# The first layer's modulation vectors as TensorE matmuls, and all low parts on VectorE

## The chip, the cores and the metric

The kernel runs on one core of a Trainium2 chip. The metric is the time of one execution on the device in microseconds (us). The core's engines are TensorE (PE, with its weight loads as PEld), VectorE (DVE), ScalarE (ACT) and GpSimd (POOL); SyncE (SP) issues most of the transfers.

## The reference, cut to what matters

Two blocks follow each other on 256 tokens of width 1024. The first is one layer of spatial gating, attention and a mixture of experts. The second has two layers on the same tokens and on 256 context tokens, each of them a feed-forward part, a mixer and a second feed-forward part. Each layer of the second block is steered by nine modulation vectors of 1024 numbers for each of two conditions, `c` and `c_ctx`:

```
mx = jnp.split(jax.nn.silu(c) @ ada_w[layer] + ada_b[layer], N_MOD, axis=-1)
mc = jnp.split((jax.nn.silu(c_ctx) @ ada_w[layer] + ada_b[layer])[None, :], N_MOD, axis=-1)
x = x + 0.5 * mx[2][:, None] * swiglu(modulate(rms_norm(x), mx[0], mx[1]), ...)
...
def modulate(h, shift, scale):
    return h * (1 + scale[:, None, :]) + shift[:, None, :]
```

`ada_w` is [2, 1024, 9216] in float32. A layer's share is 72 tiles of 512 KB, multiplied by only two vectors. All else in the reference is the same before and after.

## The kernel before, in words

**Weights in two parts.** Every weight block is a tile of 128x1024 float32 (512 KB). `W` (lines 101 to 115) loads it on SP's queue into `raw`. ScalarE copies it to `whi`, rounded to float32r (line 113), and the low part `wlo` is `raw - whi` (line 114), on VectorE or on GpSimd by a pattern of zeros and ones (`P1`, `PA`, `PB`, `PC` and so on, one for each stage). Three matmuls (lines 139 to 141) then make up one product. There are 5 buffers of `raw`, 6 of `whi` and 5 of `wlo`. A block serves 24 matmuls of 256 columns or 12 of 512 columns when 256 tokens are worked on, and twice these columns for 512 tokens.

**Stages.** By the profile's time: block 1 (0 to 400 us; the projections `w_in` and `w_u`, attention beside the first half of the gated merge, the second half, `w_out`), with the first feed-forward part of the context tokens begun at its end; the mixture of experts (to about 800 us; 32 experts with 4 blocks of `w13` and 2 of `w2` each, the context's feed-forward steps emitted between them); then of the second block's layer 0 the feed-forward part on `x` (827 to 1074 us), the mixer and the second feed-forward part over 512 tokens; then the same of layer 1, the last feed-forward part on 256 tokens alone (2227 to 2416 us).

**Modulation.** `ada(L)` (lines 832 to 875) is a generator of 72 steps. A step loads a tile `araw` of transposed `ada_w` (line 847, two buffers); GpSimd multiplies it by the condition `cb[:, 1]` into `ajk` (line 851) and ScalarE sums the rows (line 852); VectorE does product and sum for `cb[:, 0]` in one instruction (line 855). The sums are columns of `acols`. After 24 steps the bias is added and the gate rows go to scratch memory. Steps are emitted beside the main work: `W` pumps `rate` steps for each block (`R1`, `RA`, `RC`), and `need` makes up what a stage must have.

**Order.** A scheduler with a simulated time line places the instructions of each engine. Each engine and SP's queue then run in that order; an instruction that waits holds back what stands behind it. Copies of activations into `cols` (lines 838 and 845; at steps 0, 24 and 48 of layer 1, at steps 24 and 48 of layer 0 through `GT`) keep the steps behind them from being placed earlier than those activations.

**Banks.** PSUM tiles by tag: three `mm`, two `at`, two `tr` and one `ada`. The `ada` bank is also the output of attention in block 1 and in the mixers.

Of the kernel before, what the change touches and what calls it, by code (L numbers as in the profile page):

```python
# [6 lines left out]
F32 = mybir.dt.float32  # L7
F32R = mybir.dt.float32r
# [3 lines left out]
OP = mybir.AluOpType  # L12
# [18 lines left out]
PF = (1,1)  # L31
# [3 lines left out]
P1 = (0,0,0,0,0,1)  # L35
PM = (0,)
PA = (0,0,0,1)
PB = (0,1,1,1)
PC = (1,)
# [4 lines left out]
P2 = (0,1,1)  # L44
PN = (0,1,1)
PM0 = (0,1)
# [23 lines left out]
class Builder:  # L70
# [7 lines left out]
    # ------------------------------------------------------------ tiles  # L78
# [38 lines left out]
    def pump(self, n):  # L117
        """emit n steps of the work that runs beside the main chain"""
        while self.side and n > 0:
            try:  # L120
                next(self.side[0])
                n -= 1
                self.done += 1
            except StopIteration:
                self.side.pop(0)

    def need(self, L, third):
        """the modulation of layer L, up to a third, has been emitted"""
        self.pump(72 * L + 24 * third - self.done)
# [5 lines left out]
    def mm3(self, p, L, R, first, last):  # L135
        """p (+)= (Lh + Ll)^T (Rh + Rl) without the product of the two low parts."""
# [23 lines left out]
        # y <- (y * y * v * s - 3) * y = -2 * next, with the scale s of the step before  # L160
# [11 lines left out]
    def row_norm(self, x, i, g=None, use=None):  # L172
        """x[:, i] * its reciprocal root mean square (* g), in a scratch tile; use is called for each half"""
# [17 lines left out]
    def half(self, x, i):  # L191
        """the first half of the sum for a norm, before the second half of the row is there"""
# [57 lines left out]
    # ------------------------------------------------------------ program  # L250
# [45 lines left out]
    def proj_T(self, p, wb, c, hh, hl, ts, kts=range(8)):  # L296
        """p[d, tokens] of one tile of 128 output columns, weights stationary"""
# [5 lines left out]
    def block1(self):  # L303
# [3 lines left out]
        with tc.tile_pool(name="b1", bufs=1, reuse_waits="tile") as P:  # L307
# [43 lines left out]
            # w_in blocks, moving form, 4 per 512 columns: v_a 0.., k 8.., q 16.., v_b 24..  # L351
# [38 lines left out]
            # lam = exp(q1.k1) - exp(q2.k2) + 0.2  # L390
# [9 lines left out]
            # constants of the query / key / sub norms: gain * hd**-0.5, gain * (1 - lam_init)  # L400
# [5 lines left out]
            # ---- q, k, v_b  # L406
# [27 lines left out]
            # ---- differential attention  # L434
# [3 lines left out]
            def attention():  # L438
                for tt in range(2):
# [54 lines left out]
            # ---- gated merge, channel-major  # L494
# [12 lines left out]
                        # 2 sigmoid(z) = 1 + tanh(z / 2)  # L507
# [23 lines left out]
            # the context tokens' first norm  # L531
# [9 lines left out]
            # ---- x += merged @ w_out  # L541
# [7 lines left out]
    # ------------------------------------------------------------ mixture of experts  # L549
# [751 lines left out]
def prep(I):  # L1301
# [3 lines left out]
    D = {}  # L1305
# [91 lines left out]
```

## Time and profile before

| | |
|---|---|
| median of 3 runs | 2422.49 us (2419.78 to 2427.06) |
| the profiled execution: span from first to last instruction | 2426.3 us |
| its time apart from the span | not listed; the span lies among the three runs |
| mean granted TensorE clock | 0.955 |
| PE, DVE, ACT, POOL busy | 90%, 73%, 50%, 45% of the span |
| moved by DMA | 438.04 MB, mean 181 GB/s |

The busy share of an engine is a mean over stages that have different limits. The page's slices show PE at seven tenths and above nearly everywhere, DMA at nine tenths in the experts' stage only, VectorE at eight or nine tenths in block 1, the experts and the stage after them, and GpSimd busy mostly where the modulation steps run. The granted clock falls below full speed in slices where TensorE had pauses.

### The profile page before, as it was taken

The page shows a single profiled execution, that of the slowest core. Times are in us where ns is not written, and L with a number is a line of the kernel's source. Part 1 is how long each engine was busy: PE and PEld are TensorE (multiplying, and loading weights), DVE is VectorE, ACT ScalarE, POOL GpSimd, SP SyncE. Part 2 cuts the span into 40 slices and gives each one's busy share as a digit, 9 for nine tenths or more (in the row PEclk, how much of TensorE's full clock was granted, in tenths as well). Part 3 has the DMA queues.
Part 4 walks back from the last instruction along what each step waited for, and adds up shares of the span by engine and source line. Part 5 has one row for each costly group of instructions (what it writes and reads, how often), then busy time and mean ns, then how long its engine had stood idle before and what let it go on. Part 6 is the DMA issues. An engine that isn't in the chain of part 4 may idle for free. (4 is left out here: it accounts for less than half of the span.)

```text
span 2426.3 us, 32703 instructions
## 1 busy us (share of the span) xinstructions
PE 2185.9 (90%) x11890; PEld 1789.9 (74%) x11890; DVE 1762.7 (73%) x2334; ACT 1219.1 (50%) x1926; POOL 1096.8 (45%) x528
## 2 busy tenths in 40 slices
PE   7778899999999788878998999899989999888998
PEld 5657787757666677666877878688768888767997
DVE  7899878898898799999657787755874343764334
ACT  6445545888888554444635434333542222444443
POOL 5656141000000366674136989963661101414885
PEclk9899899999999899988999999999999999988999
DMA  7564365899999666663123445443453222312553
GB/s 274 168 211 154 113 215 174 315 336 326 338 322 338 244 212 232 224 203 129 49 97 130 166 156 191 171 142 105 161 169 113 96 87 87 124 66 97 187 186 114
DMA packets 121924, 438.04 MB, mean 181 GB/s; under 512 B 15072, under 2 KB 15200, under 8 KB 121632
## 3 DMA queue, kind: packets, MB, share of 16 engines
q1 hardware_dynamic: 113760, 413.19, 49.6%
q0 software_dynamic: 8000, 22.73, 2.7%
q8 instruction: 94, 1.54, 0.3%
q14 instruction: 70, 0.57, 0.1%
HBM read 429.52 MB, written 6.34 MB: 180 GB/s over the span
## 5 line engine op out<-in xcount | busy, mean ns | idle before, releaser
L114 POOL TENSOR_TENSOR wlo<-raw,whi 128x1024 fp32r<-128x1024 f32 x233 | 606.4, 2617 | 540.7 <-PE mm L141 155.3
L113 ACT ACTIVATE whi<-raw 128x1024 fp32r<-128x1024 f32 x640 | 666.1, 1054 | 325.5 <-PE mm L141 115.2
L114 DVE TENSOR_TENSOR wlo<-raw,whi 128x1024 fp32r<-128x1024 f32 x407 | 570.4, 1411 | 128.9 <-PE mm L141 55.3
L851 POOL TENSOR_TENSOR ajk<-araw,cb 128x1024 f32<-128x1024 f32 x144 | 417.2, 2897 | 288.0 <-DMA araw<-ada_w 166.9
L855 DVE SCALAR_TENSOR_TENSOR araw<-araw,cb 128x1024 f32<-128x1024 f32 x144 | 311.5, 2164 | 85.4 <-POOL ajk L851 85.4
L852 ACT ACTIVATE ajk<-ajk 128x1024 f32<-128x1024 f32 x144 | 152.3, 1058 | 261.9 <-POOL ajk L851 256.0
L140 PE MATMUL mm<-wlo,fh 128*128 128x512 f32 x616 | 247.7, 405 | 20.2 <-DVE wlo L114 13.0
L139 PE MATMUL mm<-whi,fh 128*128 128x512 f32 x616 | 246.5, 406 | 13.2 <-ACT fh L132 8.7
L141 PE MATMUL at<-hT,wlo 128*128 128x256 f32 (+1 forms) x736 | 247.5, 338 | 7.1 <-DVE wlo L114 7.1
L141 PE MATMUL mm<-whi,fl 128*128 128x512 f32 x616 | 246.5, 403 | 7.1 <-DVE fl L133 7.0
L140 PE MATMUL mm<-hT,whi 128*128 128x256 f32 (+1 forms) x736 | 245.7, 335 | 8.0 <-DVE hT L133 8.0
L139 PE MATMUL at<-hT,whi 128*128 128x256 f32 (+1 forms) x736 | 245.7, 338 | 7.9 <-DVE silu L928 7.9
L141 PE MATMUL mm<-hT,wlo 128*128 128x256 f32 (+1 forms) x736 | 244.7, 334 | 4.6 <-DVE wlo L114 4.6
L140 PE MATMUL at<-hT,whi 128*128 128x256 f32 (+1 forms) x736 | 247.3, 337 | 0.0
L139 PE MATMUL mm<-hT,whi 128*128 128x256 f32 (+1 forms) x736 | 243.2, 336 | 2.5 <-ACT hT L132 2.5
L694 POOL DMA_DIRECT2D yo<-os x64 | 31.8, 497 | 378.7 <-ACT os L693 364.2
L133 DVE TENSOR_TENSOR fl<-silu,fh 128x256 fp32r<-128x256 f32 (+1 forms) x104 | 135.8, 1309 | 48.2 <-ACT fh L132 48.2
L928 DVE TENSOR_TENSOR silu<-silu,at 128x256 f32<-128x256 f32 (+1 forms) x104 | 54.9, 528 | 147.5 <-PE at L141 144.9
L141 PEld LDWEIGHTS at<-hT,wlo 128*128 128x128 f32 x736 | 143.2, 195 | 22.5 <-DVE wlo L114 7.9
L139 PEld LDWEIGHTS at<-hT,whi 128*128 128x128 f32 x736 | 142.1, 195 | 23.5 <-DVE silu L928 8.1
L140 PEld LDWEIGHTS mm<-wlo,fh 128*128 128x128 f32 x616 | 118.7, 193 | 55.1 <-DVE wlo L114 17.5
L140 PEld LDWEIGHTS mm<-hT,whi 128*128 128x128 f32 x736 | 140.5, 191 | 24.4 <-DVE hT L133 10.0
(369 smaller groups left out, 4631.6 us busy)
## 6 DMA issues: line engine op xcount, KB each, us to landing
raw<-gu SPq DMA_DIRECT2D x220, 512.0 KB, 4.4
raw<-w SPq DMA_DIRECT2D x192, 512.0 KB, 5.2
araw<-ada_w SPq DMA_DIRECT2D x144, 512.0 KB, 3.8
raw<-dn SPq DMA_DIRECT2D x110, 512.0 KB, 4.5
raw<-w_in SPq DMA_DIRECT2D x54, 512.0 KB, 4.6
raw<-w_out SPq DMA_DIRECT2D x24, 512.0 KB, 4.1
raw<-w_gate SPq DMA_DIRECT2D x16, 512.0 KB, 4.4
raw<-w_up SPq DMA_DIRECT2D x16, 512.0 KB, 3.8
```

The source lines that it names most:

```text
L113: self.nc.scalar.activation(out=hi[:, :cols], in_=src, func=AF.Copy)
L114: eng.tensor_tensor(out=lo[:, :cols], in0=src, in1=hi[:, :cols].bitcast(F32), op=OP.subtract)
L133: self.nc.vector.tensor_tensor(out=lo, in0=src, in1=hi.bitcast(F32), op=OP.subtract)
L139: mm(p, lh, rh, start=first, stop=False)
L140: mm(p, lh, rl, start=False, stop=False)
L141: mm(p, ll, rh, start=False, stop=last)
L694: (nc.scalar if YS else nc.gpsimd).dma_start(yo[e * CAP : e * CAP + CAP, c * 512 : c * 512 + 512], os)
L851: nc.gpsimd.tensor_tensor(out=jk, in0=raw, in1=cb[:, 1], op=OP.mult)
L852: nc.scalar.activation(out=jk, in_=jk, func=AF.Copy, accum_out=acc[1])
L855: nc.vector.scalar_tensor_tensor(out=raw, in0=raw, scalar=1.0, in1=cb[:, 0], op0=OP.mult, op1=OP.mult, accum_out=acc[0])
L928: nc.vector.tensor_tensor(out=s, in0=s, in1=pgu[1][c], op=OP.mult)
```

## The change

1. **Low parts.** All patterns become `(0,)`: the 233 subtractions that GpSimd did go to VectorE. GpSimd keeps a copy of keys in the mixers and the issue of transfers.
2. **Layer 0's modulation on TensorE.** Four tiles of `ada_w0` (4 x 256 rows by 512 columns) make a group; there are 18 groups. Eight float32 matmuls take 32 stationary columns (the two conditions and 30 zeros) and 512 moving columns. They write to four partition ranges of one `ada` bank in turn (kt % 4), so that each range holds a part of the sum. ScalarE copies the bank to `e`, four small matmuls with the selection matrix `c_sel` add the parts and turn rows into columns, and one VectorE addition brings the bias.
3. **Layer 1's modulation on VectorE alone.** Both products with sums are VectorE instructions (lines 862 and 863 of the changed kernel). The conditions `cb` are loaded when layer 1 begins, into two of the `araw` buffers.
4. **Buffers.** `araw` has five buffers in place of two; `cb`, `ajk` and `arow` are gone and their contents use the ring of `araw`, as do two key tiles and a query tile in the mixers.
5. **Copies.** The copies at steps 24 and 48 of layer 0 (`GT`) are gone; layer 1 keeps its own.
6. `need` rounds up to whole groups of four steps. Comments are removed throughout, which shifts line numbers.

```diff
-PF = (1,1)
+PF = None
-P1 = (0,0,0,0,0,1)
+P1 = (0,)
...
-GT = (24,48)
...
     def need(self, L, third):
-        self.pump(72 * L + 24 * third - self.done)
+        n = max(72 * L + 24 * third, self.done)
+        self.pump(n + -n % 4 - self.done)
...
     def ada_begin(self):
-        self.cb = self.t(G, [128, 2, 1024], F32, "cb")
-        for a in range(2):
-            nc.gpsimd.dma_start(self.cb[:, a], self.A["c_rows"][a].partition_broadcast(128))
-        nc.scalar.activation(out=self.cb, in_=self.cb, func=AF.Silu)
+        self.cc = self.t(G, [128, 8, 32], F32, "cc")
+        nc.vector.memset(self.cc, 0.0)
+        c = self.load(G, "c_cols", [128, 8, 2], "ccol")
+        nc.scalar.activation(out=self.cc[:, :, 0:2], in_=c, func=AF.Silu)
+        self.sel = self.load(G, "c_sel", [128, 2], "csel")
...
         if L:
+            cb = [self.t(G, [128, 1024], F32, "araw", 5) for _ in range(2)]
+            for a in range(2):
+                nc.gpsimd.dma_start(cb[a], A["c_rows"][a].partition_broadcast(128))
+                nc.scalar.activation(out=cb[a], in_=cb[a], func=AF.Silu)
...
         for n in range(72):
-            if n in (GT, GT1)[L]:
+            if L and n in GT1:
...
-            raw = self.t(G, [128, 1024], F32, "araw", 2)
-            nc.sync.dma_start(raw, A["ada_w"][L, n])
-            jk = self.t(G, [128, 1024], F32, "ajk")
-            acc = [cols[:, a, n : n + 1] for a in range(2)]
-            if PF and n % PF[1] < PF[0]:
-                nc.gpsimd.tensor_tensor(out=jk, in0=raw, in1=cb[:, 1], op=OP.mult)
-                nc.scalar.activation(out=jk, in_=jk, func=AF.Copy, accum_out=acc[1])
+            raw = self.t(G, [128, 1024], F32, "araw", 5)
+            nc.sync.dma_start(raw, A["ada_w0"][n] if L == 0 else A["ada_w"][n])
+            if L == 0:
+                pend.append(raw)
+                if n % 4 == 3:
+                    self.ada_rows(cols, b, n // 4, pend)
+                    pend = []
             else:
-                nc.vector.scalar_tensor_tensor(out=jk, in0=raw, scalar=1.0, in1=cb[:, 1], op0=OP.mult, op1=OP.mult, accum_out=acc[1])
-            nc.vector.scalar_tensor_tensor(out=raw, in0=raw, scalar=1.0, in1=cb[:, 0], op0=OP.mult, op1=OP.mult, accum_out=acc[0])
+                jk = self.t(G, [128, 1024], F32, "araw", 5)
+                nc.vector.scalar_tensor_tensor(out=jk, in0=raw, scalar=1.0, in1=cb[1], op0=OP.mult, op1=OP.mult, accum_out=cols[:, 1, n : n + 1])
+                nc.vector.scalar_tensor_tensor(out=raw, in0=raw, scalar=1.0, in1=cb[0], op0=OP.mult, op1=OP.mult, accum_out=cols[:, 0, n : n + 1])
...
+    def ada_rows(self, cols, b, g, wf):
+        p = self.mm([128, 512], "ada")
+        for kt in range(8):
+            r = slice(kt % 4 * 32, kt % 4 * 32 + 32)
+            nc.tensor.matmul(p[r], self.cc[:, kt], wf[kt // 2][:, kt % 2 * 512 : kt % 2 * 512 + 512], start=kt < 4, stop=kt >= 4)
+        e = self.t(self.G, [128, 512], F32, "araw", 5)
+        nc.scalar.activation(out=e, in_=p, func=AF.Copy)
+        q = self.mm([128, 4, 2], "ada")
+        for c in range(4):
+            nc.tensor.matmul(q[:, c], e[:, c * 128 : c * 128 + 128], self.sel, start=True, stop=True)
+        k = slice(4 * g, 4 * g + 4)
+        nc.vector.tensor_tensor(out=cols[:, :, k], in0=q.rearrange("p c a -> p a c"), in1=b[:, None, k].to_broadcast([128, 2, 4]), op=OP.add)
```

The scheduler gives another order. Of layer 0's 72 tiles, 24 were loaded in block 1 and 48 after the experts; now 28 are loaded before the experts' stage gets going, 40 between its first 55 weight blocks, and 4 late in layer 0's mixer. SP's queue at the start of the experts, before (`w` are blocks of `w13` and `w2`, `gu` and `dn` those of the context's feed-forward part, `araw` the modulation tiles):

```order
L112 DMA raw<-gu 128x1024 x12
L112 DMA raw<-dn 128x1024 x3
L112 DMA raw<-w 128x1024 x5
L779 TENSOR_LOAD mxi
L779 ISA x2
L112 DMA raw<-w 128x1024 x3
L112 DMA raw<-dn 128x1024 x3
L112 DMA raw<-w 128x1024 x12
L112 DMA raw<-gu 128x1024 x4
```

The same place of SP's queue in the changed kernel:

```order
L111 DMA raw<-dn 128x1024
L854 DMA araw<-ada_w 128x1024 x4
L111 DMA raw<-dn 128x1024
L854 DMA araw<-ada_w 128x1024
L111 DMA raw<-w 128x1024
L854 DMA araw<-ada_w 128x1024 x3
L111 DMA raw<-w 128x1024 x6
L854 DMA araw<-ada_w 128x1024 x4
L111 DMA raw<-w 128x1024 x5
L854 DMA araw<-ada_w 128x1024
L111 DMA raw<-gu 128x1024
L854 DMA araw<-ada_w 128x1024 x3
```

In this manner it goes on to the 40th tile; behind it the queue of the experts is as before. On TensorE's own order in the changed kernel, these tiles' matmuls (`ada<-araw,cc`) stand mostly in pairs between the experts' matmuls:

```order
L139 MATMUL mm<-whi,hd 32x512
L891 MATMUL ada<-araw,cc 32x512 x2
L140 MATMUL mm<-wlo,hd 32x512
L141 MATMUL mm<-whi,hd 32x512
L139 MATMUL mm<-whi,hd 32x512
L140 MATMUL mm<-wlo,hd 32x512
L141 MATMUL mm<-whi,hd 32x512
L891 MATMUL ada<-araw,cc 32x512 x2
L145 MATMUL tr<-ident,hs 128x32 x2
```

Before, no modulation work stood between them on any engine. In layer 0's feed-forward part on `x` it is the other way round. SP's queue before, from that part's start:

```order
L112 DMA raw<-gu 128x1024 x2
L847 DMA araw<-ada_w 128x1024
L112 DMA raw<-gu 128x1024
L847 DMA araw<-ada_w 128x1024
L112 DMA raw<-gu 128x1024 x3
L847 DMA araw<-ada_w 128x1024
L112 DMA raw<-dn 128x1024
L847 DMA araw<-ada_w 128x1024
```

and in the changed kernel, from the same start up to the mixer's `w_out`:

```order
L111 DMA raw<-gu 128x1024 x6
L111 DMA raw<-dn 128x1024 x8
L111 DMA raw<-gu 128x1024 x16
L111 DMA raw<-dn 128x1024 x8
L111 DMA raw<-gu 128x1024 x12
L111 DMA raw<-dn 128x1024 x6
L111 DMA raw<-w_in 128x1024 x12
L111 DMA raw<-w_out 128x1024 x6
L854 DMA araw<-ada_w 128x1024
```

All of that part's modulation tiles have left it. Layer 1's steps stay in layer 0's second and layer 1's first feed-forward part, and there VectorE's order in the changed kernel has both products of a tile (lines 862, 863) next to the low parts (line 113):

```order
L862 SCALAR_TENSOR_TENSOR araw,acols<-araw 128x1024
L113 TENSOR_TENSOR wlo<-raw,whi 128x1024
L863 SCALAR_TENSOR_TENSOR araw,acols<-araw 128x1024
L862 SCALAR_TENSOR_TENSOR araw,acols<-araw 128x1024
L863 SCALAR_TENSOR_TENSOR araw,acols<-araw 128x1024
L952 TENSOR_TENSOR silu<-silu,at 128x512
L862 SCALAR_TENSOR_TENSOR araw,acols<-araw 128x1024
L133 TENSOR_TENSOR fl<-silu,fh 128x512
```

Before, the first of the two and the low parts of that stage were on GpSimd.

## Rows read from the trace of the kernel before

**Rows 1.** The page: busy time of each engine, share of the span, instructions.

```profile
PE 2185.9 (90%) x11890; PEld 1789.9 (74%) x11890; DVE 1762.7 (73%) x2334; ACT 1219.1 (50%) x1926; POOL 1096.8 (45%) x528
```

**Rows 2.** Windows by stage: busy us and instructions of each engine, clock, DMA share.

```profile
0.00:280.00 280.00, 211.24 (x1217) 181.00 (x1218) 245.69 (x380) 145.63 (x267) 145.25 (x71) 0.91 0.55 190
...
400.00:800.00 400.00, 381.99 (x2054) 258.13 (x2053) 352.97 (x415) 331.31 (x458) 31.79 (x64) 1.00 0.92 325
800.00:1160.00 360.00, 288.37 (x1707) 253.13 (x1706) 327.86 (x425) 172.75 (x283) 212.40 (x94) 0.90 0.58 198
1160.00:1320.00 160.00, 149.56 (x904) 127.00 (x903) 101.41 (x185) 81.28 (x184) 55.19 (x29) 0.96 0.27 85
1320.00:1840.00 520.00, 491.87 (x2186) 394.97 (x2185) 368.99 (x343) 209.97 (x315) 382.70 (x141) 0.98 0.46 157
1840.00:2080.00 240.00, 240.00 (x1028) 193.06 (x1028) 97.35 (x114) 66.78 (x85) 32.37 (x16) 1.00 0.30 97
2080.00:2240.00 160.00, 131.13 (x729) 109.04 (x728) 101.92 (x219) 73.52 (x144) 54.71 (x37) 0.87 0.28 91
2240.00:2426.00 186.00, 176.49 (x1236) 164.13 (x1234) 75.49 (x92) 79.58 (x111) 144.76 (x60) 0.98 0.49 162
```

**Rows 3.** Costliest groups of the page: xcount | busy us, mean ns | idle before, releaser.

```profile
L114 POOL TENSOR_TENSOR wlo<-raw,whi 128x1024 fp32r<-128x1024 f32 x233 | 606.4, 2617 | 540.7 <-PE mm L141 155.3
...
L114 DVE TENSOR_TENSOR wlo<-raw,whi 128x1024 fp32r<-128x1024 f32 x407 | 570.4, 1411 | 128.9 <-PE mm L141 55.3
L851 POOL TENSOR_TENSOR ajk<-araw,cb 128x1024 f32<-128x1024 f32 x144 | 417.2, 2897 | 288.0 <-DMA araw<-ada_w 166.9
```

**Rows 4.** Groups by form, VectorE, 840 to 1080 us.

```profile
L114 DVE TENSOR_TENSOR wlo<-raw,whi 128x1024 fp32r<-128x1024 f32 x44 | 83.1, 1901 | 1.1 <-PE mm L141 0.6 <-ACT whi L113 0.5
```

**Rows 5.** Groups by form, VectorE, 1320 to 1600 us.

```profile
L855 DVE SCALAR_TENSOR_TENSOR araw<-araw,cb 128x1024 f32<-128x1024 f32 x45 | 131.3, 2918 | 45.3 <-POOL ajk L851 45.3
L133 DVE TENSOR_TENSOR fl<-silu,fh 128x512 fp32r<-128x512 f32 x16 | 26.1, 1635 | 9.8 <-ACT fh L132 9.8
```

**Rows 6.** Groups by form, VectorE, 440 to 800 us.

```profile
L114 DVE TENSOR_TENSOR wlo<-raw,whi 128x1024 fp32r<-128x1024 f32 x220 | 265.7, 1219 | 40.0 <-ACT whi L113 35.9 <-ACT fh L132 0.6 <-PE at L729 0.5
```

**Rows 7.** Line 855: ns min/median/max, first and last start.

```profile
L855 DVE SCALAR_TENSOR_TENSOR araw<-araw,cb x144: 1209/1226/3495, 28.1 to 1815.8; 128x1024 f32<-128x1024 f32 x144
```

**Rows 8.** Waits of TensorE, 0 to 280 us: us in total, times, longest.

```profile
PE tr L145 <- DVE T L183: 14.3, 2, 8.4
PE mm L140 <- DVE wlo L114: 13.9, 7, 3.1
```

**Rows 9.** TensorE in order of time: start us, us, form, pieces merged.

```profile
2171.95 1.03 PE L1152 MATMUL mm<-fftc,pf 128*128 128x256 f32 x4
2172.63 0.58 PE L1096 MATMUL at<-araw,qT 128*128 128x512 f32 x1
```

**Rows 10.** The same view, 192 to 194 us.

```profile
192.43 1.10 PE L453 MATMUL at<-A,A 64*128 64x128 f32 x8
193.46 0.39 PE L140 MATMUL mm<-S,whi 128*128 128x256 f32 x1
```

**Rows 11.** The same view, 2182 to 2185 us.

```profile
2182.49 1.89 PE L1110 MATMUL ada<-v,aT 128*128 128x64 f32 x16
2184.22 0.50 PE L145 MATMUL tr<-ident,e 128*128 128x128 f32 x3
```

**Rows 12.** DMA issues: line, engine, count, KB each, us to landing.

```profile
araw<-ada_w SPq DMA_DIRECT2D x144, 512.0 KB, 3.8
```

**Rows 13.** Windows of two feed-forward passes over 256 tokens.

```profile
827.00:1074.00 247.00, 210.04 (x1337) 190.06 (x1336) 226.57 (x213) 122.61 (x194) 155.36 (x56) 0.91 0.63 213
2227.00:2416.00 189.00, 189.00 (x1327) 177.08 (x1327) 74.39 (x81) 85.66 (x118) 148.76 (x61) 0.99 0.47 157
```

**Rows 14.** Chain that ended last, 2100 to 2160 us: start us, us, what.

```profile
2118.05 2.29 DVE rsy L159
...
2128.93 2.71 DVE xs L1066
```

More of the change, by code (lines that the diff above doesn't have):

```diff
@@ L34 @@
 KD = 3
-P1 = (0,0,0,0,0,1)
+P1 = (0,)
 PM = (0,)
-PA = (0,0,0,1)
-PB = (0,1,1,1)
-PC = (1,)
+PA = (0,)
+PB = (0,)
+PC = (0,)
 PO = "ada"
@@ L43 @@
 NA = 3
-P2 = (0,1,1)
-PN = (0,1,1)
-PM0 = (0,1)
+P2 = (0,)
+PN = (0,)
+PM0 = (0,)
 R2 = .3
@@ L50 @@
 AB = 2
-GT = (24,48)
 CUT = (0,3,5,8,11)
 LAG = 1
-PU = (1,)
+PU = (0,)
 KF = 0
@@ L824, in ada_begin @@
         nc, G = self.nc, self.G
-        self.cb = self.t(G, [128, 2, 1024], F32, "cb")
-        for a in range(2):
-            nc.gpsimd.dma_start(self.cb[:, a], self.A["c_rows"][a].partition_broadcast(128))
-        nc.scalar.activation(out=self.cb, in_=self.cb, func=AF.Silu)
+        self.cc = self.t(G, [128, 8, 32], F32, "cc")
[3 more added lines that the diff above has]
+        self.sel = self.load(G, "c_sel", [128, 2], "csel")
     def ada(self, L):
         nc, A, G = self.nc, self.A, self.G
-        cb = self.cb
         d2 = self.dr.tile([2, 3, 1024], F32, tag="ada2", bufs=2, name="ada2")
@@ L841, in ada @@
         nc.gpsimd.dma_start(b, A["ada_b"][L])
+        pend = []
         for n in range(72):
-            if n in (GT, GT1)[L]:
+            if L and n in GT1:
                 gate = self.x[:, 0, 0:48] if self.gate is None else self.gate[:, 0:48]
                 nc.vector.tensor_copy(cols[:, :, n : n + 24], gate.rearrange("p (a b) -> p a b", a=2))
-            raw = self.t(G, [128, 1024], F32, "araw", 2)
-            nc.sync.dma_start(raw, A["ada_w"][L, n])
-            jk = self.t(G, [128, 1024], F32, "ajk")
-            acc = [cols[:, a, n : n + 1] for a in range(2)]
-            if PF and n % PF[1] < PF[0]:
-                nc.gpsimd.tensor_tensor(out=jk, in0=raw, in1=cb[:, 1], op=OP.mult)
-                nc.scalar.activation(out=jk, in_=jk, func=AF.Copy, accum_out=acc[1])
-            else:
-                nc.vector.scalar_tensor_tensor(out=jk, in0=raw, scalar=1.0, in1=cb[:, 1], op0=OP.mult, op1=OP.mult, accum_out=acc[1])
-            nc.vector.scalar_tensor_tensor(out=raw, in0=raw, scalar=1.0, in1=cb[:, 0], op0=OP.mult, op1=OP.mult, accum_out=acc[0])
+            raw = self.t(G, [128, 1024], F32, "araw", 5)
[4 more added lines that the diff above has]
+                    self.ada_rows(cols, b, n // 4, pend)
+                    pend = []
+            else:
+                jk = self.t(G, [128, 1024], F32, "araw", 5)
+                nc.vector.scalar_tensor_tensor(out=jk, in0=raw, scalar=1.0, in1=cb[1], op0=OP.mult, op1=OP.mult, accum_out=cols[:, 1, n : n + 1])
+                nc.vector.scalar_tensor_tensor(out=raw, in0=raw, scalar=1.0, in1=cb[0], op0=OP.mult, op1=OP.mult, accum_out=cols[:, 0, n : n + 1])
             if n % 24 == 23:
@@ L858, in ada @@
                 k = slice(24 * t, 24 * t + 24)
-                nc.vector.tensor_tensor(out=cols[:, :, k], in0=cols[:, :, k], in1=b[:, None, k].to_broadcast([128, 2, 24]), op=OP.add)
+                if L:
+                    nc.vector.tensor_tensor(out=cols[:, :, k], in0=cols[:, :, k], in1=b[:, None, k].to_broadcast([128, 2, 24]), op=OP.add)
                 k = slice(24 * t + 8, 24 * t + 16)
@@ L868, in ada @@
                     self.tr(p[:, a], cols[:, a, k])
-                r = self.t(G, [8, 2, 128], F32, "arow")
+                r = self.t(G, [8, 2, 128], F32, "araw", 5)
                 nc.scalar.activation(out=r, in_=p, func=AF.Copy)
@@ L874, in ada @@
         self.dbg(f"mods{L}", cols)
+    def ada_rows(self, cols, b, g, wf):
+        nc = self.nc
+        p = self.mm([128, 512], "ada")
[9 more added lines that the diff above has]
+        nc.vector.tensor_tensor(out=cols[:, :, k], in0=q.rearrange("p c a -> p a c"), in1=b[:, None, k].to_broadcast([128, 2, 4]), op=OP.add)
     def seg(self, cols, a, s):
@@ L967, in mixer @@
             v = self.t(P, [128, 4, 128], F32, "v")
-            kT = [self.t(self.G, [128, 2, 512], F32R, "araw", 2) for _ in range(2)]
+            kT = [self.t(self.G, [128, 2, 512], F32R, "araw", 5) for _ in range(2)]
             S = {}
@@ L1071, in queries @@
                         qr = q8
-                    qc = self.t(self.G, [128, 8, 2, 64], F32R, "ajk")
+                    qc = self.t(self.G, [128, 8, 2, 64], F32R, "araw", 5)
                     self.split(qr, qc[:, :, 0], qc[:, :, 1])
@@ L1340, in prep @@
     D["c_rows"] = np.concatenate([I["c_2"], I["c_ctx_2"][None]])
-    D["ada_w"] = np.stack([np.ascontiguousarray(w.T).reshape(72, 128, 1024) for w in I["ada_w_2"]])
+    D["ada_w0"] = mov(I["ada_w_2"][0], 512)
+    D["ada_w"] = np.ascontiguousarray(I["ada_w_2"][1].T).reshape(72, 128, 1024)
+    D["c_cols"] = np.ascontiguousarray(D["c_rows"].reshape(2, 8, 128).transpose(2, 1, 0))
+    sel = np.zeros((4, 32, 2), f)
+    sel[:, 0, 0] = sel[:, 1, 1] = 1
+    D["c_sel"] = sel.reshape(128, 2)
     D["ada_b"] = np.stack([col(v) for v in I["ada_b_2"]])
```

## The prediction, made before the changed kernel ran

> **What bounds the kernel now.** I read the page's busy times first [rows 1]: TensorE 90%, VectorE 73%, GpSimd 45%. The mean hides the stages, so the windows come next [rows 2]. In each, TensorE's busy time times its granted clock is about the work it did at full speed; the rest of the window is lost to it. For 0 to 280 us that is 280 - 211 x 0.91 = 88 us lost; for 800 to 1160, 360 - 288 x 0.90 = 100; for 1160 to 1320, 160 - 150 x 0.96 = 16; for 1320 to 1840, 520 - 492 x 0.98 = 38; for 2080 to 2240, 160 - 131 x 0.87 = 46; for the last 186 us 13. From 1840 to 2080 nothing is lost: 240 us of it hold 1028 matmuls, so one of 512 columns takes 0.233 us. The experts (400 to 800) lose 18, and there the transfers are at their limit too: share 0.92, 325 GB/s. So TensorE is the bound of the second half, TensorE and the transfers together bound the experts, and two stages, block 1 and 800 to 1160, lose 188 us of the 319.
>
> Why these two? VectorE is busy 246 of 280 us and 328 of 360 us there [rows 2], and part of that is not its own work. A low part costs it 1.22 us in the experts, where GpSimd only issues transfers [rows 6], but 1.90 us between 840 and 1080 [rows 4]. The product with sum of line 855 takes 1.21 us at least and 3.50 at most [rows 7]; between 1320 and 1600, beside a GpSimd that never rests, its mean is 2.92 and that of `fl` 1.64 [rows 5]. GpSimd needs 2.62 us for a low part and 2.90 for a product [rows 3]. Instructions with two inputs on chip are stretched while GpSimd computes. TensorE then waits for low parts and for chains of small VectorE instructions [rows 8]; in the layer-1 mixer a step on one number per partition or eight takes 2.29 us and a gain of 512 numbers 2.71 [rows 14].
>
> **What goes from GpSimd to VectorE.** 233 low parts [rows 3] at 1.22 us add 284 us to VectorE. The 407 it had cost 1.41 each; at 1.22 they give back 77. Of line 855's 144 products (2.16 us would be 311 in all; at 1.22 they are 176) the count stays 144: 72 of layer 0 go, 72 of layer 1 come. So VectorE's total hardly moves, but it moves in place: in block 1 24 products go and 25 low parts come, so its 246 us fall to some 190 of 280, and between 800 and 1160 the 43 products vanish. Bounds for the price of a low part: 1.22 with GpSimd still, 1.90 with it at work; I take 1.22, since nothing but transfers is left on GpSimd but for two key copies in each mixer.
>
> **What the 18 groups cost TensorE.** No row shows a matmul on 32 columns in float32. The nearest: a float32 matmul appears as two passes; four passes of 256 columns start 0.68 us before the next form [rows 9], three intervals of 0.216 and a rest, so a pass of 512 columns is 0.43 us. One behind the other a group's 16 passes would take 6.9 us. The nearest row for tiles of the array side by side is line 453, whose two halves use different rows of it: eight passes of 256 columns take 1.03 us [rows 10] where the spacing above gives 7 x 0.216 + 0.03 = 1.54. A third is saved: each matmul's second pass runs beside the next one's first. I take that for columns too: 16 passes 4.6 us. The four selections are eight passes of 0.108 us (16 take 1.73 [rows 11]), 0.9 us. A group is 5.5 us, 18 are 99. Ends: nothing saved, 7.8 us and 140; four at once, 1.7 + 0.9 = 2.6 us and 47.
>
> These prices rest on rows; what the Trainium skill says of it stands beside them. Its page TensorEngine Tiling (Array Packing), section Theoretical Speedup, gives up to four times for a dimension of 32; by that the 18 groups would be the 47 us end. Its section Key Properties says that changing the tiling mode drains the engine, which speaks against 32-column pairs strewn among full matmuls. The trace shows a third saved and a next matmul 1.03 us after eight passes, so neither the full factor nor a long drain; for columns no row shows either.
>
> **Block 1.** Lost now 88. Of this 14 is the first norm chain [rows 8], which stays at about 12; waits for low parts (14 by VectorE) nearly go; of the softmax and norm chains half. The clock's part, 211 x 0.09 = 19, halves as pauses go. I take 40 us back (bounds: 0, if TensorE's new waits replace the old; 60, if only start and clock stay). Six groups stand in this stage, 33 us; some wait with attention for the same `ada` bank, so I cover none. Net -7. A seventh group, at the stage's end, counts half: +3.
>
> **The experts.** Here the order puts 40 tiles, ten groups. On the transfers: 0.524 MB at 325 GB/s is 1.61 us, 64 us in all. On TensorE: ten groups, 55 us, with little lost to hide them in. Both limits are near full and grow together, so I take the larger: +64. Bounds: +32, if the share rises from 0.92 to 1.00; +90, if passes don't overlap (78) and the one `ada` bank makes groups wait for ScalarE's copy and VectorE's addition (about 1 us a group). On SP a modulation load that waits for a buffer holds back the experts' blocks behind it; five `raw` buffers stand ahead.
>
> **Layer 0's first feed-forward part.** The order leaves no modulation in it. The same 66 blocks on the same 256 tokens run at the kernel's end without any: 189 us there, 247 here [rows 13]. I take all of the difference, -58. VectorE then has its 74 us of the later pass and 66 x 1.22 = 81 for low parts, 155 of 189. Bounds: -45 if these make waits, -62.
>
> **Mixers and the rest.** The two mixers' chains lose contention: the two records above alone are over by some 2 us each, and a chain has a handful. -9 for layer 0's (its stages lose 16 and the rest of 100 - 58), -8 for layer 1's, -3 at the end; the last group, among the mixer's `w_out`, +3. Bounds for the three together -30 and +5, since low parts now stand between the links.
>
> **Layer 1's 72 tiles** (1320 to 1840): GpSimd's product goes, VectorE's doubles. The order sets 24 tiles beside 19 blocks, 1.25 a block. A block of 512 tokens is 24 x 0.233 = 5.6 us of TensorE. VectorE has 1.22 for the low part, 1.25 x 2 x 1.22 = 3.05 for products, up to 0.8 for `fl`: 5.1. It fits with 0.5 us to spare. Two `araw` buffers hold the conditions, so three are left: a tile's load starts when the products of the second tile before it end, and has one tile's period, about 4 us, for a latency of 3.8 [rows 12]. I take +3 (bounds -15 and +58, below).
>
> **Sum.** -7 + 3 + 64 - 58 - 9 - 8 - 3 + 3 + 3 = -12 us against the profiled span of 2426.3, which is 3.8 above the median 2422.5: 2414 there, 2410 for the median.
>
> **Rivals.**
> A. Four columns at once, 2.6 us a group: block 1 gets back 17, the rest 3, the experts stay with their transfers; and block 1's pauses go but for the start, 10 more. 2410 - 30 = 2380. For it: the four ranges are written in turn; against: second passes follow in the same range.
> B. Slower: VectorE becomes the bound under layer 1's tiles. It now waits itself for each tile's load (before, GpSimd did, 166.9 us of its idle time [rows 3]), and behind it stand low parts and `silu`, for which TensorE waits. The point: 0.5 us a block is free, 0.4 a tile. A load issued late on SP's queue makes the wait 1.2 us: 72 x 0.8 = 58. 2468. Against: five `wlo` buffers let TensorE run on for a while, and the tiles come in three bursts.
> C. The tiles don't run side by side as the change means them to: 7.8 us a group. Block 1 +14, the experts +24 with the bank's waits, the other two groups +4: 2452. Against: line 453's rows.
>
> **How the numbers follow.** Chances: forecast 0.50 (own range 2388 to 2430), A 0.20, B 0.16, C 0.14. A measurement of this kernel can tell about 0.3%, 7 us. Below 2415 lie two thirds of the forecast's case and nearly all of A: 0.52. Within 2415 to 2430: a quarter of the forecast's, a little of the others: 0.16. Above: 0.32. The range goes from A less 35 us, where block 1 gives all, to B: 2345 to 2468.
>
> **What would show it.** Low parts at 1.22 us everywhere; experts about 64 us longer at a share of 0.92 or more, with ten groups of 5 to 6 us of TensorE in their first third; the feed-forward part of layer 0 at 190 us; block 1 near its old length; VectorE's waits for `araw` under 0.4 us a tile. Wrong: experts that grow by under 40 or over 90, a feed-forward part over 205, or VectorE at 95% between 1320 and 1840 with TensorE waiting for low parts.

## The result, and the profile after

The changed kernel takes 2321.4 us (median; 2320.0 to 2322.2) against 2421.1 us for the kernel before on the same chip: a ratio of 0.958, 95% interval 0.957 to 0.960. The prediction had the sign, but its 2410 us is 89 us too high and the time lies below its range. The profiled execution's span is 2318.2 us, 108.1 shorter than before.

The page after answers to [rows 1, 3, 12]; its first row is the busy time of each engine, the second row is VectorE's low parts (count | busy us, mean ns | idle before), the third a transfer (count, size, us to landing):

```profile
PE 2211.2 (95%) x12322; PEld 1779.3 (77%) x12322; DVE 1548.9 (67%) x2581; ACT 1087.1 (47%) x1658; POOL 80.7 (3%) x153
...
L113 DVE TENSOR_TENSOR wlo<-raw,whi 128x1024 fp32r<-128x1024 f32 x640 | 776.5, 1221 | 275.3 <-PE mm L141 143.4
...
araw<-ada_w SPq DMA_DIRECT2D x144, 512.0 KB, 4.6
```

All 640 low parts are VectorE's, each at 1.22 us, and its total still fell by 214 us. GpSimd computes nothing to speak of.

For the stages I take marks that both traces have: block 1 ends with VectorE's last `x<-mm,x`; a feed-forward part begins with its first matmul `at<-hT` and, where a mixer follows, ends with its last down matmul. Lengths in us; "layer 1's tiles" are layer 0's second and layer 1's first feed-forward part.

| stage | before | changed | difference | predicted |
|---|---|---|---|---|
| block 1 | 348.6 | 307.6 | -41.0 | -7 + 3 |
| experts | 479.2 | 533.0 | +53.8 | +64 |
| layer 0, first feed-forward | 246.0 | 187.8 | -58.2 | -58 |
| layer 0, mixer | 214.1 | 186.4 | -27.7 | -9 + 3 |
| layer 1's tiles | 793.1 | 773.2 | -19.9 | +3 |
| layer 1, mixer | 147.1 | 132.4 | -14.7 | -8 |
| last feed-forward, end | 198.2 | 197.9 | -0.3 | -3 |
| sum | 2426.3 | 2318.2 | -108.1 | -12 |

Windows of the changed kernel, which answer to [rows 2, 13] (start:end, length, busy us of TensorE, weight loads, VectorE, ScalarE, GpSimd, clock, DMA share, GB/s):

```profile
0.00:280.00 280.00, 259.92 (x1706) 217.09 (x1707) 195.25 (x407) 149.01 (x261) 9.62 (x21) 0.98 0.61 213
308.00:841.00 533.00, 496.92 (x2731) 328.25 (x2731) 415.56 (x578) 369.11 (x513) 39.92 (x74) 0.97 0.87 313
840.00:1028.00 188.00, 188.00 (x1326) 176.07 (x1325) 116.38 (x158) 90.40 (x123) 1.60 (x3) 0.99 0.57 182
1028.00:1215.00 187.00, 180.34 (x1051) 149.92 (x1050) 122.60 (x313) 92.73 (x207) 8.26 (x17) 1.00 0.26 87
1240.00:1760.00 520.00, 507.01 (x2266) 411.62 (x2267) 363.25 (x555) 142.97 (x185) 3.11 (x6) 0.99 0.50 161
1970.00:2130.00 160.00, 141.34 (x786) 117.47 (x785) 109.11 (x266) 78.57 (x155) 11.28 (x19) 0.94 0.32 104
```

Worked as before, TensorE loses 280 - 260 x 0.98 = 25 us in the first 280 (88 before), 18 between 1240 and 1760 (38 in the matching 520), 27 in layer 1's mixer (46). What it still waits for in the first 280 us answers to [rows 8] (total, times, longest):

```profile
PE tr L145 <- DVE T L183: 8.3, 1, 8.3
PE ada L891 <- ACT cc L829: 6.2, 1, 6.2
PE ada L891 <- ACT hft L479: 1.9, 2, 1.2
```

The start is left, and the waits for low parts are gone. The small instructions of layer 1's mixer, against [rows 14]:

```profile
2021.37 0.23 DVE L159 TENSOR_SCALAR rsy<-rsv 128x8 int32<-128x8 int32 x2
...
2027.85 0.69 DVE L1090 TENSOR_TENSOR xs<-xs,qgain 128x512 f32<-128x512 f32 x1
```

Two such steps now end within 0.23 us where one took 2.29, and the gain takes 0.69 in place of 2.71. In the kernel before, the slow step stood beside low parts on GpSimd (start us, us):

```profile
2116.86 8.20 POOL L114 TENSOR_TENSOR wlo<-raw,whi 128x1024 fp32r<-128x1024 f32 x3 [0.94 <-ACT whi L113]
2117.97 2.38 DVE L159 TENSOR_SCALAR rsy<-rsv 128x8 int32<-128x8 int32 x1
```

It reads one array on chip, not two, so the prediction's sentence that instructions with two inputs on chip are stretched is true but not the whole.

A piece of a modulation group among the experts (start us, us, form, records):

```profile
410.82 0.40 PE L139 MATMUL mm<-whi,hd 128*32 128x512 f32 x1
411.15 1.05 PE L891 MATMUL ada<-araw,cc 128*32 128x512 f32 x4
412.13 0.41 PE L140 MATMUL mm<-wlo,hd 128*32 128x512 f32 x1
```

One tile's two matmuls are four passes on two ranges of columns; the next matmul starts 0.98 us later. The order places most groups in such pieces. The experts' stage holds eleven groups' matmuls: the ten whose tiles it loads, and one whose tiles were loaded before it. All 18 groups' matmuls hold TensorE 65 us from a piece's start to the next other matmul, 3.6 a group; with a selection of 0.85 that is 4.5.

### The profile page after: what moved, and what is told of

Its sections match the earlier page's. It is cut to its first block, busy times and chain, and to the rows that moved or that the text cites. A ratio compares the mean times of both kernels' runs of the same rounds, so it can differ in the third digit from the quotient of the medians.

```text
span 2318.2 us, 32701 instructions
## 1 busy us (share of the span) xinstructions
PE 2211.2 (95%) x12322; PEld 1779.3 (77%) x12322; DVE 1548.9 (67%) x2581; ACT 1087.1 (47%) x1658; POOL 80.7 (3%) x153
## 5 line engine op out<-in xcount | busy, mean ns | idle before, releaser
L113 DVE TENSOR_TENSOR wlo<-raw,whi 128x1024 fp32r<-128x1024 f32 x640 | 776.5, 1221 | 275.3 <-PE mm L141 143.4
L140 PE MATMUL at<-hT,whi 128*128 128x256 f32 (+1 forms) x736 | 244.2, 333 | 0.0
L140 PE MATMUL mm<-wlo,fh 128*128 128x512 f32 x616 | 241.4, 395 | 0.4 <-DVE wlo L113 0.3
L139 PE MATMUL at<-hT,whi 128*128 128x256 f32 (+1 forms) x736 | 241.2, 332 | 0.0
L140 PEld LDWEIGHTS mm<-hT,whi 128*128 128x128 f32 x736 | 141.3, 192 | 23.8 <-DVE hT L133 9.2
L139 PEld LDWEIGHTS mm<-hT,whi 128*128 128x128 f32 x736 | 139.1, 192 | 19.3 <-ACT hT L132 4.5
L141 PEld LDWEIGHTS mm<-hT,wlo 128*128 128x128 f32 x736 | 141.3, 192 | 14.6
L141 PEld LDWEIGHTS at<-hT,wlo 128*128 128x128 f32 x736 | 140.1, 190 | 14.7
L140 PEld LDWEIGHTS at<-hT,whi 128*128 128x128 f32 x736 | 140.1, 190 | 14.7
L139 PEld LDWEIGHTS at<-hT,whi 128*128 128x128 f32 x736 | 138.4, 190 | 14.7
L132 ACT ACTIVATE fh<-silu 128x256 fp32r<-128x256 f32 (+1 forms) x104 | 52.3, 503 | 203.6 <-DVE silu L952 203.6
L912 DVE TENSOR_TENSOR gadd<-mm,grow 128x512 f32<-128x512 f32 x100 | 68.8, 688 | 117.4 <-PE mm L141 116.5
L139 PEld LDWEIGHTS mm<-whi,fh 128*128 128x128 f32 x616 | 116.1, 188 | 30.8 <-ACT os L693 1.7
L141 PEld LDWEIGHTS mm<-whi,fl 128*128 128x128 f32 x616 | 116.1, 188 | 27.3
```

Of the source, the lines that this page charges most:

```text
L113: eng.tensor_tensor(out=lo[:, :cols], in0=src, in1=hi[:, :cols].bitcast(F32), op=OP.subtract)
L132: self.nc.scalar.activation(out=hi, in_=src, func=AF.Copy)
L139: mm(p, lh, rh, start=first, stop=False)
L140: mm(p, lh, rl, start=False, stop=False)
L141: mm(p, ll, rh, start=False, stop=last)
L912: nc.vector.tensor_tensor(out=t, in0=p, in1=g[:, cs], op=OP.mult)
```

## The experiments

Two theories stood at the start. Theory 1: VectorE freed of a computing GpSimd makes the gain. Theory 2: the first layer's products off VectorE make it. A ratio is to the kernel before on the same chip, where its median was 2421 to 2425 us; the 95% interval stands beside it.

**Low parts back on GpSimd** (changed kernel):

```
-P1 = PA = PB = PC = P2 = PN = PM0 = PU = (0,)
+P1 = (0,0,0,0,0,1); PA = (0,0,0,1); PB = (0,1,1,1)
+P2 = PN = (0,1,1); PM0 = (0,1); PC = PU = (1,)
```

> Layer 0's modulation stays on TensorE and layer 1's two products on VectorE, as in the changed kernel; only the low parts go back to the old shares between GpSimd and VectorE. Theory 1 (the gain beyond the forecast is VectorE freed of a computing GpSimd): most of it is lost again, 2370 to 2410 us, with low parts on VectorE above 1.4 us. Theory 2 (the gain is the first layer's modulation off VectorE, whatever GpSimd does): 2325 to 2345 us.

Measured 2411.1 us, ratio to before 0.995 (0.993 to 0.997): 90 of the 100 us gained are lost again, 1 us above theory 1's range. TensorE still did the first layer's modulation, so theory 2 is out. But theory 1's sign came only in part: VectorE's low parts took 1.28 us on average (1.35 in block 1, 1.44 between 1050 and 2212 us), not above 1.4. So this run doesn't tell whether VectorE was stretched or TensorE waited for GpSimd's slower low parts (2.60 us each); the run with idle work, below, goes into that.

**All low parts on VectorE, modulation as before** (kernel before, the lists at (0,)):

> The kernel before with all low parts on VectorE and nothing else: modulation as it was, its first product on GpSimd and the second on VectorE. Theory 1: some of the gain comes by this alone, 2360 to 2400 us, limited by GpSimd's 144 products, which still stretch VectorE. Theory 2: no gain, 2410 to 2450 us, because VectorE is too full between 0 and 280 and in layer 0's feed-forward part.

2380.5 us, 0.983 (0.980 to 0.985), in theory 1's range. In layer 0's first feed-forward part nothing was gained (247.7 us), and VectorE shows why (count | busy us, mean ns | idle before):

```profile
L114 DVE TENSOR_TENSOR wlo<-raw,whi 128x1024 fp32r<-128x1024 f32 x63 | 110.6, 1761 | 0.9 <-PE mm L141 0.9
L855 DVE SCALAR_TENSOR_TENSOR araw<-araw,cb 128x1024 f32<-128x1024 f32 x42 | 68.4, 1630 | 7.0 <-POOL ajk L851 7.0
L133 DVE TENSOR_TENSOR fl<-silu,fh 128x256 fp32r<-128x256 f32 x22 | 28.4, 1291 | 1.0 <-ACT fh L132 1.0
```

Beside GpSimd's products alone, VectorE's low parts take 1.76 us there.

**GpSimd still, all modulation on VectorE** (kernel before, lists at (0,) and the first product moved):

```
-PF = (1,1)
+PF = None
```

> As the run with the low parts on VectorE, and both products of every modulation tile on VectorE too, so that GpSimd only issues transfers; TensorE computes no modulation. Theory 1: 2330 to 2370 us, near the changed kernel although VectorE has 88 us more (72 products of 1.22). Theory 2: 2400 to 2450 us, VectorE near 95% in layer 0's stages.

2293.9 us, 0.946 (0.944 to 0.948): faster than the changed kernel, without any modulation on TensorE, and below theory 1's range. VectorE makes 144 products more than before and is yet less busy:

```profile
PE 2147.6 (94%) x11890; PEld 1769.6 (77%) x11890; DVE 1693.1 (74%) x2855; ACT 1074.4 (47%) x1638; POOL 79.2 (3%) x151
```

(1762.7 us before [rows 1].) So the whole gain comes with GpSimd still, and the move to TensorE as the change makes it costs 27 us. This run also takes 144 row sums from ScalarE (1074 us busy against 1219); what that is worth was not told apart. Where the time goes, the stages tell (us):

| stage | before | changed | GpSimd still | gated (below) | idle work (below) |
|---|---|---|---|---|---|
| block 1 | 348.6 | 307.6 | 311.4 | 308.7 | 322.9 |
| experts | 479.2 | 533.0 | 473.9 | 472.6 | 540.0 |
| layer 0, first feed-forward | 246.0 | 187.8 | 193.3 | 216.9 | 187.7 |
| layer 0, mixer | 214.1 | 186.4 | 213.2 | 188.3 | 202.7 |
| layer 1's tiles | 793.1 | 773.2 | 770.8 | 767.6 | 806.8 |
| layer 1, mixer | 147.1 | 132.4 | 133.7 | 132.2 | 151.3 |
| last feed-forward, end | 198.2 | 197.9 | 198.0 | 197.5 | 215.4 |

With GpSimd still, the experts keep their length; the changed kernel adds 59 us there and takes 32 back in layer 0's next two stages, where VectorE had 48 tiles' products.

**Work on GpSimd whose result nobody reads** (changed kernel):

```
+if m: nc.gpsimd.tensor_tensor(out=src, in0=src, in1=src, op=OP.subtract)
```

after VectorE's low part, for the 233 blocks of the old lists.

> The changed kernel; in addition GpSimd subtracts each of the 233 weight blocks whose low part it used to make from itself, after VectorE has made that low part. Nobody reads the result; only the block's raw buffer comes free later. So GpSimd computes as often and about where it did, but no engine waits for its output. Theory F (the loss was VectorE stretched by a computing GpSimd): of the 90 us that lie between the changed kernel (2321) and the one with the low parts on GpSimd (2411), more than half come back, 2366 to 2400 us, with low parts on VectorE over 1.5 us in the feed-forward parts. Theory G (the loss was TensorE waiting for low parts that take GpSimd 2.6 us): 2318 to 2335 us.

2426.1 us, 1.001 (1.000 to 1.002): all of the gain is gone, beyond theory F's range. Low parts on VectorE took over 1.5 us in the last feed-forward part alone (2.35); in layer 0's first, with 18 subtractions on GpSimd, they took 1.24 and the stage lost nothing (187.7 us), in layer 1's tiles 1.43. The last feed-forward part shows the mechanism. VectorE there with the idle work, and GpSimd's rows:

```profile
L112 DVE TENSOR_TENSOR wlo<-raw,whi 128x1024 fp32r<-128x1024 f32 x61 | 142.2, 2351 | 3.3 <-PE mm L142 2.7 <-PE at L142 0.5
L134 DVE TENSOR_TENSOR fl<-silu,fh 128x256 fp32r<-128x256 f32 x22 | 21.9, 996 | 4.8 <-ACT fh L133 4.8
L914 DVE TENSOR_TENSOR x<-x,gadd 128x512 f32<-128x512 f32 x12 | 13.5, 1122 | 0.2
...
L913 DVE TENSOR_TENSOR gadd<-mm,grow 128x512 f32<-128x512 f32 x12 | 8.2, 684 | 0.8 <-PE mm L142 0.5
```

```profile
L114 POOL TENSOR_TENSOR raw<-raw 128x1024 f32<-128x1024 f32 x61 | 136.1, 2243 | 68.8 <-DVE wlo L112 42.7 <-ACT hft L236 14.0 <-issue 12.1
```

and VectorE in the changed kernel's last part:

```profile
L113 DVE TENSOR_TENSOR wlo<-raw,whi 128x1024 fp32r<-128x1024 f32 x61 | 74.3, 1223 | 40.6 <-PE mm L141 26.7 <-PE mm L140 12.1 <-PE at L141 0.5
L133 DVE TENSOR_TENSOR fl<-silu,fh 128x256 fp32r<-128x256 f32 x22 | 9.3, 422 | 4.8 <-ACT fh L132 4.8
...
L913 DVE TENSOR_TENSOR x<-x,gadd 128x512 f32<-128x512 f32 x12 | 8.3, 689 | 0.2
L912 DVE TENSOR_TENSOR gadd<-mm,grow 128x512 f32<-128x512 f32 x12 | 8.3, 688 | 10.6 <-PE mm L141 10.6
```

What reads two operands on chip is stretched (1.22 to 2.35, 0.42 to 1.00, 0.69 to 1.12 us); `gadd`, which reads one of its two from PSUM, is not (0.69 and 0.68). The Trainium skill says the same: SBUF — State Buffer, section Who interferes with whom, has a VectorE instruction with two SBUF inputs contend with a GpSimd instruction that reads SBUF, and one with at most one such input, outside the two-port modes, not. The trace agrees for these rows. In this part VectorE had become the bound: 3.3 us idle before 61 low parts, 40.6 without the idle work. The raw buffers also come free some 2 us later in this kernel, and ScalarE then waits for weights, which it doesn't in the changed kernel's last part:

```profile
ACT whi L111 <- DMA raw<-gu: 14.5, 11, 2.9
```

With VectorE that full, this hardly sets the part's length; how much of the 105 us late buffers add in the other stages was not told apart.

**All matmuls of a group on one range of columns** (changed kernel):

```
-matmul(p[r], ..., start=kt < 4, stop=kt >= 4)      # r: 32 columns by kt % 4
+matmul(p[0:32], ..., start=kt == 0, stop=kt == 7)
```

> The changed kernel with all eight matmuls of a group on one range of 32 columns, so that none can run beside another; the result is the same. Theory A (tiles on different columns run fully side by side): sixteen passes one behind the other, 6.9 us a group in place of 3.6 on average, 18 groups 59 us more of TensorE; 20 to 40 us of it show, 2340 to 2365 us, since the experts also wait for transfers. Theory C (they never ran side by side): no difference, 2318 to 2326 us.

2360.2 us, 0.973 (0.971 to 0.976): theory A, 39 us slower. A whole group, serial, and below it one in the gated kernel with its four ranges filled:

```profile
375.44 7.05 PE L890 MATMUL ada<-araw,cc 128*32 128x512 f32 x16
382.43 0.62 PE L713 MATMUL tr<-oh,A 128*128 128x256 f32 x3
```

```profile
833.91 1.92 PE L894 MATMUL ada<-araw,cc 128*32 128x512 f32 x16
835.77 0.50 PE L139 MATMUL mm<-whi,fh 128*128 128x512 f32 x1
```

Sixteen passes take 6.99 us to the next matmul on one range, 1.86 on four: 3.8 times as fast.

**Layer 0's later tiles held back** (changed kernel; at steps 24 and 48 the stationary condition is rewritten with 0 x the feed-forward part's input):

```
+if L == 0 and n in (24, 48):
+    nc.vector.scalar_tensor_tensor(out=cc, in0=self.gate, scalar=0.0, in1=cc, op0=OP.mult, op1=OP.add)
```

> The changed kernel with layer 0's second and third thirds of the modulation held back until its first feed-forward part has its input, as before the change: 11 of the 18 groups then stand in the feed-forward part and the mixer, none among the experts. Theory P (the 40 tiles cost what they do because the experts' transfers are at their limit): the experts fall by some 54 us, the two later stages grow by less than the groups' 11 x 4.5 = 50 us of TensorE: 2285 to 2312 us. Theory Q (a group costs TensorE's time wherever it stands): 2313 to 2330 us.

2285.5 us, 0.943 (0.941 to 0.945): theory P, and faster than both kernels. Twelve groups stand in the two later stages, not eleven. The experts fall by 60 us; the feed-forward part grows by 29 for ten groups:

```profile
781.00:998.00 217.00, 217.00 (x1566) 189.05 (x1565) 120.44 (x172) 96.73 (x134) 3.31 (x7) 0.99 0.73 256
```

TensorE is full there, and a group costs its time alone, 1.86 + 0.85 = 2.7 us: the loads had come early, so the groups are not split.

**What the 40 tiles cost among the experts.** First without their loads, then without their matmuls (changed kernel):

```
-nc.sync.dma_start(raw, A["ada_w0"][n])                    # n = 28 .. 67
+(no load; the matmuls read the identity)
```

> The changed kernel without the loads of layer 0's tiles 28 to 67; their matmuls stay and read the identity matrix instead, so the modulation they give is wrong. Theory D (the transfers bind the experts): they fall by most of their 54 us, 2270 to 2290 us. Theory E (TensorE binds them): no more than 15 us go, 2306 to 2322 us.

```
-self.ada_rows(cols, b, n // 4, pend)                      # n = 28 .. 67
+nc.vector.tensor_copy(cols[:, :, k], b[:, None, k] ...)
```

> The changed kernel with the loads of layer 0's tiles 28 to 67, but without their matmuls, copies and selections; the modulation of these tiles is left out. Theory D: the loads alone cost what all did, 2306 to 2322 us. Theory E: ten groups of 4.5 us go, 2270 to 2285 us.

2279.5 us (0.940, 0.938 to 0.941) and 2293.5 us (0.946, 0.944 to 0.947): the first in theory D's range, the second in neither. The experts' windows, matmuls only and loads only:

```profile
309.00:810.00 501.00, 476.91 (x2734) 326.44 (x2733) 414.15 (x580) 370.02 (x515) 41.19 (x74) 0.98 0.83 291
```

```profile
309.00:813.00 504.00, 455.18 (x2491) 313.73 (x2490) 413.69 (x565) 366.58 (x505) 40.75 (x74) 0.96 0.90 330
```

Against the gated kernel's 472.6 us, the matmuls alone add 28, the loads alone 32, both 60. Neither theory holds for both runs: the two costs add, and neither hides the other. That they add exactly is not shown. Without the loads the groups are less cut up (their matmuls hold TensorE 32 us there, 41 in the changed kernel), and the gated kernel's second profile has 479.5 us for this stage.

**Only the first third on TensorE** (the kernel with GpSimd still, all else on VectorE):

> The kernel with GpSimd still and all modulation on VectorE, with only layer 0's first third moved to TensorE (six groups, in block 1). If block 1 gains what it gained in the changed kernel over that one (41 against 37 us), 2285 to 2293 us; if the groups only take TensorE's time, 2294 to 2310 us.

2306.1 us, 0.952 (0.950 to 0.953), in the second range and slower than with none. Block 1 takes 318 us there against 311.4, some 7 of the 10 us between the two profiled spans. This kernel holds two modulation tiles on chip where the changed one holds five; whether that is the reason was not tried.

**Four pieces of 256 columns a tile** (gated kernel):

```
-matmul(p[kt % 4], ..., 512 columns)
+matmul(p[kt % 2 * 2 + h], ..., 256 columns)   for h in (0, 1)
```

> The gated kernel (2285.5 us), with each tile of layer 0's modulation cut into four pieces of 256 columns on four ranges of TensorE's columns, in place of two of 512 on two; same products. If four ranges run side by side and two ranges leave half of the array idle, a tile of two passes of 512 (0.98 us to the next matmul) becomes two of 256 with the same change of form, about 0.4 us: 72 x 0.5 = 36 us less of TensorE, of which most shows where TensorE is the bound: 2250 to 2272 us. If changing to 32 columns and back sets the price, 2280 to 2290 us.

2287.7 us, 0.944 (0.941 to 0.946): no gain. The time lies in the second range, but not for its reason. My premise was wrong: the gated kernel's groups already fill four ranges (14 of 18 stand in one piece), and such a group has 1.86 us to the next matmul in both. Pieces of one tile do shrink, from 0.98 to 0.57 us, but there are few.

**Side by side, in five rounds**: GpSimd still against gated.

> The kernel with GpSimd still and all modulation on VectorE once more, in more rounds and on one chip with the gated kernel, to tell what the move to TensorE is worth by itself. If TensorE is worth what its stages gained over this one (block 1 some 3 us, the mixer 25, less 24 in the feed-forward part, 6 elsewhere), the gated kernel is 6 to 12 us faster; if their difference was between chips, they agree within 4 us.

> The gated kernel on the same chip as the run with all modulation on VectorE: 6 to 12 us faster than that one, or within 4 us of it, as told there.

2296.3 us (0.947, 0.945 to 0.949) and 2287.2 us (0.943, 0.941 to 0.944). So the gated kernel is some 9 us faster, 0.4%, as the expectation's stages had it; the two intervals only just stay apart. That is what modulation on TensorE is worth if the tiles stay where they were before, as far as these kernels show it: they differ in their buffers too (two modulation tiles on chip, and five).

## Why the prediction was wrong

**Low parts, 1.22 us everywhere.** Right, to the nanosecond of the row: 1221.

**The first feed-forward part of layer 0, -58.** Right (-58.2), and so was its pattern, the kernel's last pass. But the reason given, that the order leaves no modulation in it, is not what counted: with GpSimd still and the tiles left there the part falls to 193.3 us, 53 of the 58, and with the low parts alone moved it stays at 247.7. What had to leave it was GpSimd's products. VectorE was busy 116 us there, not the 155 of the sum.

**A group at 5.5 us.** Measured 4.5, by two errors that nearly cancel. The first is a misread row. I took [rows 10] for passes of 256 columns; it says 64x128, and for 128 columns the same working (half of 0.216 a pass) gives 0.79 us one behind the other, so its 1.03 us show no saving at all. The same line has passes of 256 columns later in block 1 of the kernel before:

```profile
231.44 1.14 PE L453 MATMUL at<-A,A 64*128 64x256 f32 x8
232.51 0.39 PE L139 MATMUL mm<-S,whi 128*128 128x256 f32 x1
```

Eight such passes have 1.07 us to the next matmul, where eight of 0.216 us are 1.73: two at a time, with some 0.2 us beside (an estimate: 1.07 less four times 0.216). By that row sixteen passes on four ranges are 4 x 0.43 + 0.2 = 1.9 us, and a dense group measured 1.86. Four ranges run 3.8 times as fast as one, as rival A had it; the Trainium skill's factor of up to four (TensorEngine Tiling (Array Packing), section Theoretical Speedup) agrees. The second error is that the order cuts most groups into pieces of two ranges, each 0.98 us, which brings 18 groups to 81 us, near my 99 by luck. Rival A's 2.6 us is what the gated kernel's groups cost.

**The experts, +64.** Measured +54, within its bounds, by a wrong rule: "Both limits are near full and grow together, so I take the larger". The loads, priced at 64, cost 32 alone, the matmuls 28, and they add; that the sum came near 64 is luck. Against the same experts with GpSimd still it is +59 to +60. The tiles also stand in the experts' first part, where the share of the transfers is 0.84, not the 0.92 that I took for the whole stage:

```profile
350.00:515.00 165.00, 155.16 (x822) 85.87 (x820) 98.21 (x145) 90.52 (x130) 7.57 (x15) 0.96 0.84 318
```

Over all of the stage the share is 0.87, before (349 to 828 us) as after.

**Where it failed: what TensorE gets back.** The step is "I take 40 us back" with "I cover none" of block 1's groups, and with it "-9 for layer 0's", "-8 for layer 1's" and "+3" for layer 1's tiles. Against -15 predicted for these four (-4, -6, -8 and +3, their groups counted) the trace shows -103: 88 of the 96 us that the sum missed.

Block 1 shortened by 41 us with six groups in it. Its whole stage before, changed, and with GpSimd still (columns as in the windows above):

```profile
0.00:348.60 348.60, 279.84 (x1712) 245.29 (x1713) 292.19 (x438) 182.81 (x318) 159.07 (x77) 0.93 0.54 184
0.00:307.60 307.60, 287.52 (x1851) 240.74 (x1852) 213.59 (x427) 162.90 (x275) 13.37 (x28) 0.98 0.63 215
0.00:311.40 311.40, 270.90 (x1706) 240.90 (x1707) 261.03 (x517) 160.02 (x269) 13.37 (x28) 0.93 0.63 212
```

TensorE lost 88 us of it before and 26 in the changed kernel: 62 back, more than the bound of 60. With GpSimd still and no groups, block 1 is 37 shorter, near the 40, and TensorE still loses 59. So the six groups, priced at 33, cost this stage nothing: with them it is 4 us shorter still. Whether they ran in TensorE's pauses, or were paid for by the products that left VectorE (261 us busy against 214), was not told apart.

The other three are the size of the stretch. Layer 1's tiles gave 20 us, and 22 with GpSimd still; layer 1's mixer 15, and 13. Layer 0's mixer gave 28 with one group in it, but 1 with GpSimd still and modulation products kept on VectorE there, so it needed both parts of the change. I had seen the stretch in the rows and priced it for low parts and line 855 only ("VectorE's total hardly moves"). These two did as priced: together they grew by 70 us (284 - 77 - 135 = 72 by my terms). But VectorE's total fell by 214, so 284 us came from what I put at nothing, the other instructions, such as these before and, below, in the changed kernel:

```profile
L889 DVE TENSOR_TENSOR x<-x,gadd 128x512 f32<-128x512 f32 x56 | 80.9, 1445 | 1.5
L133 DVE TENSOR_TENSOR fl<-silu,fh 128x256 fp32r<-128x256 f32 x60 | 72.5, 1211 | 21.0 <-ACT fh L132 21.0
```

```profile
L913 DVE TENSOR_TENSOR x<-x,gadd 128x512 f32<-128x512 f32 x56 | 38.6, 689 | 1.1
L133 DVE TENSOR_TENSOR fl<-silu,fh 128x256 fp32r<-128x256 f32 x60 | 25.2, 421 | 11.6 <-ACT fh L132 11.6
```

For layer 1's tiles I even weighed a loss, because the products double; yet at 1.22 us two of them take less than one did beside GpSimd [rows 5]:

```profile
L113 DVE TENSOR_TENSOR wlo<-raw,whi 128x1024 fp32r<-128x1024 f32 x50 | 61.0, 1222 | 34.8 <-PE mm L141 30.6 <-PE at L141 2.9 <-PE mm L140 1.0
L863 DVE SCALAR_TENSOR_TENSOR araw<-araw 128x1024 f32<-128x1024 f32 x31 | 37.8, 1219 | 0.2
L862 DVE SCALAR_TENSOR_TENSOR araw<-araw 128x1024 f32<-128x1024 f32 x30 | 36.7, 1222 | 16.2 <-DMA araw<-ada_w 16.2
L133 DVE TENSOR_TENSOR fl<-silu,fh 128x512 fp32r<-128x512 f32 x17 | 11.7, 687 | 2.8 <-ACT fh L132 2.8
```

**Rival B** came half: VectorE does wait for tiles,

```profile
DVE araw L862 <- DMA araw<-ada_w: 31.6, 28, 3.4
```

31.6 us over 72 tiles, 0.44 each, just over the 0.4 that I gave as the point. But VectorE is busy for 363 of the 520 us, and TensorE waits there for no low part and no `silu`; its longest wait in total is

```profile
PE mm L140 <- DVE hT L133: 7.3, 5, 2.4
```

**Rival C** is out, by the run with one range.

None of the rivals was the one that came true: that the part of the change I counted as neutral for VectorE carries all of the gain, and the part that gives the change its name costs 27 us where the order puts it.

## What to carry to other kernels

An engine beside which another's instructions take longer costs more than its own work shows: price every instruction it stretches, the short links of chains too, and try a version with it still before giving it work. When a change has two parts, run each alone: here one gave 130 us and the other took 27, and held back to its old place it would have given 9. Work that needs two resources near their limits can pay for both; eleven groups' matmuls with ten groups' loads cost 54 to 60 us among the experts, and ten whole groups 29 where transfers had room. Read the shape in a row before its time: 64x128 taken for 256 columns hid a price that the trace held.

## What was not expected of the hardware

GpSimd work whose result nobody reads cost 105 us of 2321, late buffers included. In the kernel before, even an instruction on eight numbers per partition was stretched beside a computing GpSimd (2.29 us, against 0.23 for two in the changed kernel). Four float32 matmuls on four ranges of 32 columns run at 3.8 times the rate of one range, and going to that form and back costs some 0.2 us (an estimate): in the piece shown above the first of them starts 0.33 us after the matmul before, where 0.23 is usual, and 16 passes have 1.86 us to the next matmul where four rounds at 0.43 would be 1.72.
